# Down projection of a feed-forward: which loads wait behind a split of weights, and the order of the final product

## The chip, the core and the metric

The kernel runs on one core of a Trainium2 chip. The metric is device time in microseconds (us), from the start of the program to its end. Lower is better. The core has TensorE (PE, matrix products), VectorE (DVE), ScalarE (ACT), GpSimd (POOL) and SyncE (SP), each with its own instruction queue that runs in order, and 16 DMA engines that all loads share.

## The reference, cut to what matters

Two layers, each of them a feed-forward, a mixer and a second feed-forward, each followed by a residual and a layer norm, on 512 tokens of width 1024 in float32. A feed-forward is a SwiGLU of width 2816:

```python
def swiglu_ffn(x, w_gu, w_down):
    a, u = jnp.split(x @ w_gu, 2, axis=-1)
    return (jax.nn.silu(a) * u) @ w_down

for l in range(DEPTH):
    x = layer_norm(ALPHA*x + 0.5*swiglu_ffn(x, ffn1_w_gu[l], ffn1_w_down[l]), ln1_g[l], ln1_b[l])
    x = layer_norm(ALPHA*x + hybrid_mixer(x, w_in[l], w_out[l], ...), ln2_g[l], ln2_b[l])
    x = layer_norm(ALPHA*x + 0.5*swiglu_ffn(x, ffn2_w_gu[l], ffn2_w_down[l]), ln3_g[l], ln3_b[l])
```

So there are four feed-forwards, each with a product by `w_down` (2816x1024) at its end: the down projection. The last of them writes the output.

## The kernel before, in words

**Precision.** Every float32 operand is split in a high part (a cast on ACT, L165) and a low part (a subtract on DVE, L166), and every product is three matmuls (`mm3`: high x high on L174, high x low on L175, low x high on L176). The tile names tell what is split: `uh`/`ul` are the two parts of a unit of weights (128x1024), `xh`/`xl` the two parts of an operand from the tokens' side.

**Down projection.** Of the 22 chunks of 128 features in `hT`, 20 go through seven products of blocks instead of eight (a Strassen scheme over two halves of the features, two halves of the tokens and two halves of the 1024 output columns). In the code's names they run in the order p2, p1, p5, p6, p3, p7, p4. Each product has five groups, `seventh` computes one group, and a group is 12 matmuls of 512 columns (two PSUM banks, two chunks of features, three matmuls). The last two chunks, the tail (`down`, `tail(t)`), are ordinary products with their own raw weights. `tail(t)` also calls `norm(t)` for token tile t (0 to 3). In program order: p2, p1, p5, p6, p3, p7, then `tail(0)` and `tail(1)`, then p4 (banks of token tiles 2 and 3), then `tail(2)` and `tail(3)`.

**Weights' side of the seven products.** `R` tiles hold blocks of `w_down`, loaded by SP (L363). The products need sums of blocks, and these sums are made by DMA: after a group of p1, p5, p6 or p3 has been split, POOL issues a load that adds another block onto the same piece of `R` (L374, `accum_op=add`, 512 KB each, 20 in each down projection). The groups of p5 use what p1's groups added, those of p6 what p5's added, those of p4 what p6's added, and those of p7 what p3's added. `R[0,...]` serves p1, p5, p6 and p4; `R[1,...]` serves p3 and p7. p2 uses plain raw tiles (L386).

**Order of loads.** `Weights` holds the items (units of weights) of the whole program in order. `pump` emits splits up to `LOOK` (6) items ahead of the consumer, with 6 unit buffers, so a unit's split waits until the unit six places earlier has been used up by PE. There are two raw tiles; after each item `pump` looks through all later items for the next raw tile to load until two are held. `load_ln` loads gain and shift of the norm (two loads of 512 KB into 128 partitions). SP issues all plain loads in program order. The dependencies between instructions are turned into semaphore waits by the framework.

Of the kernel before, what the change touches and what calls it, by code (L numbers as in the profile page):

```python
# [7 lines left out]
F32 = mybir.dt.float32  # L8
# [10 lines left out]
P = 128  # L19
# [10 lines left out]
GROUPS = 5  # L30
# [2 lines left out]
PAIRS = [(m, min(4, HALF - m)) for m in range(0, HALF, 4)]  # L33
SEVEN = (2, 3, 4, 5, 6, 7, 8, 9, 10)
UBUFS = 6
LOOK = 6
DELAY = (5, 4, 9, 9)
STEPS = ((4, 2, 2), (3, 2, 3), (3, 3, 2), (3, 2, 2))

QA, KA, VA, QR, KR, VR, GR = 0, 512, 640, 768, 1280, 1792, 2304  # L40

NOSYNC = mybir.DependencyInfo(mybir.DependencyClass.NoSync, mybir.DependencyReason.DATA)


class Weights:
# [9 lines left out]
    def pump(self, most=None):  # L55
        while self.emitted < len(self.items) and self.emitted < self.taken + LOOK:
            if most is not None and self.emitted >= most:
                return
            raw, load, pool, cut = self.items[self.emitted]
            if pool is None and self.out >= UBUFS:  # L60
                return
            if raw is not None:
                self.load(raw, load)
            if pool is None:
                self.out += 1
                hi, lo = self.T.units()
            else:
                hi, lo = pool()
            self.ready.append(cut(self.raws.get(raw), hi, lo))
            self.emitted += 1  # L70
            held = sum(self.last[r] >= self.emitted for r in self.raws)
            for r2, l2, _, _ in self.items[self.emitted :]:
                if held == 2:
                    break
                if r2 is not None and r2 not in self.raws:
                    self.load(r2, l2)
                    held += 1
# [20 lines left out]
class Trunk:  # L98
    def __init__(self, tc, ctx):
        self.tc, self.nc = tc, tc.nc  # L100
        self.n = 0
        self.now = 0
        self.pin = True
        self.tasks = []
        self.later = []
        self.halves = 2
        nc = self.nc
        self.base = ctx.enter_context(tc.tile_pool(name="base", bufs=1))
        self.rawp = ctx.enter_context(tc.tile_pool(name="rawp", bufs=2))
        self.unit = ctx.enter_context(tc.tile_pool(name="unit", bufs=UBUFS))  # L110
        self.small = ctx.enter_context(tc.tile_pool(name="small", bufs=3))
        self.psum = ctx.enter_context(tc.tile_pool(name="psum", bufs=8, space=PSUM))
        self.ident = self.base.tile([P, P], F32, name="ident")
        make_identity(nc, self.ident)
        self.mhalf = self.base.tile([P, 8], F32, name="mhalf")
        nc.vector.memset(self.mhalf, -0.5)
        self.xh = self.base.tile([P, KC, SEQ], F32R, name="xh")
        self.xl = self.base.tile([P, KC, SEQ], F32R, name="xl")
        self.Y = self.base.tile([P, NT, D], F32, name="Y")
# [43 lines left out]

    def split(self, hi, lo, src):
        a = self.nc.scalar.copy(hi, src)  # L165
        b = self.nc.vector.tensor_sub(lo, src, hi.bitcast(F32))  # L166
        if self.pin:
            self.tc.keep_in_program_order(a)
            self.tc.keep_in_program_order(b)

    def mm3(self, out, a, b, start, stop, **kw):
        (ah, al), (bh, bl) = a, b
# [11 lines left out]
    def cols_item(self, w, c0, key):  # L184

        def load():
            v = self.raw().rearrange("p (k c) -> p k c", k=KC)
            src = w[:, c0 : c0 + 256].rearrange("(k p) c -> p k c", p=P)
            if self.later is not None:
                self.later.append(lambda: self.nc.sync.dma_start(v[:, :, P:], src[:, :, P:]))  # L190
                for k0 in range(0, KC, KC // (1 if self.later[1:] else 2)):
                    k1 = k0 + KC // (1 if self.later[1:] else 2)
                    self.nc.sync.dma_start(v[:, k0:k1, :P], src[:, k0:k1, :P])
            else:
                self.nc.sync.dma_start(v, src)
            return v

        def cut(c):
            def go(v, hi, lo):
                hv, lv = (t.rearrange("p (k c) -> p k c", k=KC) for t in (hi, lo))  # L200
                src, h = v[:, :, c * P : (c + 1) * P], KC // 2
                if self.halves:
                    self.halves -= 1
                    self.split(hv[:, :h], lv[:, :h], src[:, :h])
                    self.rest = lambda: self.split(hv[:, h:], lv[:, h:], src[:, h:])
                    if not self.halves:
                        self.rest()
                else:
                    self.split(hv, lv, src)
                return hv, lv  # L210
            return go

        return [(key, load, None, cut(c)) for c in range(2)]
# [50 lines left out]
    def rows_item(self, w, r0, key, pools, heads=False):  # L264

        def load():
            v = self.raw().rearrange("p (c n) -> p c n", c=2)
            if heads:
                for kv in range(2):
                    q0 = kv * 256 + r0 // 2  # L270
                    self.nc.sync.dma_start(v[kv * HD : (kv + 1) * HD],
                                           w[q0 : q0 + P, :].rearrange("(c p) n -> p c n", p=HD))
            else:
                self.nc.sync.dma_start(v, w[r0 : r0 + 256, :].rearrange("(c p) n -> p c n", p=P))
            return v

        def cut(c):
            def go(v, hi, lo):
                self.split(hi, lo, v[:, c, :])
                return hi, lo  # L280
            return go

        return [(key, load, pools[c], cut(c)) for c in range(2)]
# [63 lines left out]
    def down_items(self, w, key, tail):  # L347
# [4 lines left out]
        R = {}  # L352
# [5 lines left out]
        def begin(i, m, place, go):  # L358
            def f(*args):
                k0, n = PAIRS[m]  # L360
                pool, tag = place()
                R[i, m] = pool.tile([P, n, 512], F32, tag=tag, name=self.nm("R"), bufs=2)
                self.nc.sync.dma_start(R[i, m], rows(i, i, k0, n))  # L363
                return go(*args)
            return f

        def cut(t, g, *more):
            def go(v, hi, lo):
                hv, lv = (t_.rearrange("p (k c) -> p k c", k=2) for t_ in (hi, lo))
                src = R[t, g // 2][:, g % 2 * 2 : g % 2 * 2 + 2, :]  # L370
                self.split(hv, lv, src)
                for i, j in more:
                    self.tc.keep_in_program_order(
                        self.nc.gpsimd.dma_start(src, rows(i, j, g * 2, 2), accum_op=ALU.add))  # L374
                return hv, lv
            return go
# [94 lines left out]
    def load_ln(self, pool, g, b, tag="ln", bufs=None):  # L471
        kw = {} if bufs is None else {"bufs": bufs}
        gb = pool.tile([P, 2, D], F32, tag=tag, name=self.nm("ln"), **kw)
        self.nc.sync.dma_start(gb[:, 0, :], g.partition_broadcast(P))
        self.nc.sync.dma_start(gb[:, 1, :], b.partition_broadcast(P))
        return gb[:, 0, :], gb[:, 1, :]

    def norm(self, t, halves, gb, out=None, delay=4, scale=(ALPHA, ALPHA)):
# [29 lines left out]
    def ffn(self, g_, b, out=None):  # L508
        nc, tc, W = self.nc, self.tc, self.W
        with ExitStack() as ctx:  # L510
# [147 lines left out]
            pool = self.fpool = ctx.enter_context(tc.tile_pool(name=self.nm("ffnd"), bufs=1))  # L658
            acc = [[self.ps() for _ in range(2)] for _ in range(NT)]

            gb = self.load_ln(pool, g_, b)
            calls = [0]

            def part(m, i, j):
# [5 lines left out]
            def operand(src):  # L670


                calls[0] += 1
                k, h = ((4, 0), (0, 0), (0, 1), (4, 1))[calls[0] % 4 if calls[0] < 20 else 2]
                f = src.shape[1]
                hh, hl = (v[:, k : k + f, h * 256 : (h + 1) * 256] for v in (self.xh, self.xl))
                self.split(hh, hl, src)
                return [(hh[:, q : q + 2], hl[:, q : q + 2]) for q in range(0, f, 2)]
# [35 lines left out]
                for m in ms:  # L714
                    yield from operand(part(m, 1, 1))

            def seventh(banks, u, h, new):

                for i, b_ in enumerate(banks):
                    ts = slice(i * P, (i + 1) * P)  # L720
                    for f in range(2):
                        self.mm3(b_, (h[0][:, f, ts], h[1][:, f, ts]), (u[0][:, f, :], u[1][:, f, :]),
                                 new and f == 0, False, skip_group_check=True)
                self.step()

# [30 lines left out]
            for n, (banks, new, more) in enumerate((  # L756
# [3 lines left out]
                if n == 6:  # L760
                    last = [take() for _ in range(TAIL)]
                    self.pend = []
                    for t in range(2):
                        tail(t)
                for g in range(GROUPS):
                    u, h = take()
                    seventh(banks, u, h, new and g == 0)
                    if more and g == GROUPS - 1:
                        into(banks, *more)
                    W.done(2 if n == 0 and g == 1 else 1)  # L770
            for t in range(2, NT):
                tail(t)


    def big(self, shape, dt=F32):
# [385 lines left out]
```

## Time and profile before

| | us |
|---|---|
| median of three runs | 1786.18 |
| lowest and highest of the three | 1784.37, 1790.02 |
| the profiled execution, its own time | 1784.17 |
| its span, first to last instruction | 1782.4 |
| TensorE busy | 1758.7 |
| VectorE busy | 1414.1 |
| ScalarE busy | 926.9 |

The profile tells when each instruction ran, what ended its wait, and what DMA moved; 1.8 us of the profiled execution lie outside its span. A matmul's shown duration overlaps that of the next, so the pace of TensorE is read from the distance of starts. The granted clock says which of its two levels TensorE ran at: 1.00 is 2.4 GHz.

### The profile page before, as it was taken

What the parts mean: (1) busy time and instruction counts of PE and PEld (TensorE: products, weight loads), DVE (VectorE), ACT (ScalarE), POOL (GpSimd) and SP (SyncE); (2) the same over time, 40 slices, a digit from 0 to 9 for tenths busy, and PEclk for the clock granted to TensorE, in tenths of its full rate; (3) what the DMA queues carried; (4) which work ended last, traced back from release to release, by engine and by line L of the source; (5) the groups of instructions that cost most, each with busy time, mean ns of one, the idle gap of its engine ahead of it and who ended that gap; (6) DMA issues with size and microseconds to landing.
All of it is one profiled execution on the core that took longest, in us unless ns stands there. A gap on an engine that the chain in (4) does not pass through costs nothing.

```text
span 1782.4 us, 29182 instructions
## 1 busy us (share of the span) xinstructions
PE 1758.7 (99%) x11930; PEld 1603.4 (90%) x11930; DVE 1414.1 (79%) x1975; ACT 926.9 (52%) x1456; POOL 181.8 (10%) x152
## 2 busy tenths in 40 slices
PE   9999999999999999999999999999999999999997
PEld 9999987897789999997899999789877899999886
DVE  7888878956757888887988888888567587888886
ACT  5455546478712455555435556454696234555561
POOL 0000023111111000013100000221111110000131
PEclk9999999999999999999999999999999999999999
DMA  6334399222222243279322334972233122334891
GB/s 189 95 104 134 120 248 188 90 84 88 76 74 71 85 129 95 96 246 227 83 84 97 104 95 154 255 146 90 84 95 95 48 95 95 96 101 137 233 180 47
DMA packets 163765, 216.34 MB, mean 121 GB/s; under 512 B 5168, under 2 KB 116528, under 8 KB 163632
## 3 DMA queue, kind: packets, MB, share of 16 engines
q1 hardware_dynamic: 141872, 172.55, 30.2%
q0 software_dynamic: 21760, 41.95, 12.9%
q8 instruction: 93, 1.52, 0.4%
q14 instruction: 40, 0.33, 0.1%
HBM read 212.38 MB, written 2.10 MB: 120 GB/s over the span
## 4 chain that ended last, share of the span: by engine, by line
PE 79%; issue 10%; DMA 4%; DVE 3%; POOL 2%; ACT 1%; POOLq 0%; SPq 0%; DVEq 0%; ACTq 0%
PE ps L176 25%; PE ps L174 25%; PE ps L175 25%; DMA R<-in_ffn_w_down_dram 2%; POOL R L374 1%; DVE ul L166 1%; PE ps L461 1%; DMA raw<-in_ffn_w_gu_dram 1%; POOL sw L932 1%; PE ps L1040 1%; ACT uh L165 1%; PE ps L988 0%; PE ps L1002 0%; PE ps L1036 0%; DVE hT L596 0%
## 5 line engine op out<-in xcount | busy, mean ns | idle before, releaser
L174 PE MATMUL ps<-xh,uh 128*128 128x256 f32 (+1 forms) x1616 | 482.2, 298 | 0.0
L176 PE MATMUL ps<-xh,ul 128*128 128x256 f32 (+1 forms) x1616 | 479.4, 297 | 0.8 <-DVE ul L166 0.7
L175 PE MATMUL ps<-xl,uh 128*128 128x256 f32 (+1 forms) x1616 | 478.5, 296 | 0.2 <-DVE xl L166 0.2
L165 ACT CAST uh<-raw 128x1024 fp32r<-128x1024 f32 (+1 forms) x274 | 237.6, 886 | 229.0 <-PE ps L175 134.4
L174 PE MATMUL ps<-Th,uh 128*128 128x256 f32 x1152 | 319.1, 277 | 0.0
L175 PE MATMUL ps<-Tl,uh 128*128 128x256 f32 x1152 | 318.7, 277 | 0.0
L176 PE MATMUL ps<-Th,ul 128*128 128x256 f32 x1152 | 318.3, 276 | 0.0
L176 PEld LDWEIGHTS ps<-xh,ul 128*128 128x128 f32 x1616 | 307.9, 191 | 9.9 <-DVE ul L166 1.4
L174 PEld LDWEIGHTS ps<-xh,uh 128*128 128x128 f32 x1616 | 307.9, 191 | 9.8 <-issue 1.6
L175 PEld LDWEIGHTS ps<-xl,uh 128*128 128x128 f32 x1616 | 308.0, 191 | 7.9 <-DVE xl L166 0.4
L166 DVE TENSOR_TENSOR ul<-raw,uh 128x1024 fp32r<-128x1024 f32 (+1 forms) x274 | 273.5, 1012 | 42.0 <-ACT uh L165 41.2
L176 PE MATMUL ps<-uh,xl 128*128 128x512 f32 x720 | 283.2, 393 | 9.3 <-DVE xl L166 9.3
L174 PE MATMUL ps<-uh,xh 128*128 128x512 f32 x720 | 285.4, 396 | 0.5 <-ACT xh L165 0.5
L175 PE MATMUL ps<-ul,xh 128*128 128x512 f32 x720 | 282.0, 392 | 0.0
L165 ACT CAST uh<-S 128x1024 fp32r<-128x1024 f32 x144 | 151.1, 1050 | 149.0 <-PE ps L175 145.1
L166 DVE TENSOR_TENSOR ul<-S,uh 128x1024 fp32r<-128x1024 f32 x144 | 175.9, 1222 | 59.7 <-ACT uh L165 59.1
L175 PEld LDWEIGHTS ps<-Tl,uh 128*128 128x128 f32 x1152 | 216.7, 188 | 0.0
L174 PEld LDWEIGHTS ps<-Th,uh 128*128 128x128 f32 x1152 | 216.7, 188 | 0.0
L176 PEld LDWEIGHTS ps<-Th,ul 128*128 128x128 f32 x1152 | 216.3, 188 | 0.0
L374 POOL DMA_DIRECT2D R<-in_ffn_w_down_dram x80 | 97.1, 1217 | 1046.1 <-DVE ul L166 719.6
L165 ACT CAST uh<-R 128x1024 fp32r<-128x1024 f32 x120 | 124.4, 1047 | 125.0 <-DMA R<-in_ffn_w_down_dram 92.9
L166 DVE TENSOR_TENSOR ul<-R,uh 128x1024 fp32r<-128x1024 f32 x120 | 144.7, 1220 | 54.6 <-ACT uh L165 54.4
(143 smaller groups left out, 2372.7 us busy)
## 6 DMA issues: line engine op xcount, KB each, us to landing
raw<-in_ffn_w_gu_dram SPq DMA_DIRECT2D x86, 1024.0 KB, 5.6
R<-in_ffn_w_down_dram POOLq DMA_DIRECT2D x80, 512.0 KB, 8.4
raw<-in_w_in_dram SPq DMA_DIRECT2D x18, 1024.0 KB, 5.3
R<-in_ffn_w_down_dram SPq DMA_DIRECT2D x16, 1024.0 KB, 11.2
raw<-in_ffn_w_down_dram SPq DMA_DIRECT2D x12, 1024.0 KB, 5.4
R<-in_ffn_w_down_dram SPq DMA_DIRECT2D x8, 512.0 KB, 10.5
raw<-in_w_in_dram SPq DMA_DIRECT2D x8, 512.0 KB, 7.9
raw<-in_w_out_dram SPq DMA_DIRECT2D x8, 512.0 KB, 6.1
```

Source lines behind the costliest of these rows:

```text
L165: a = self.nc.scalar.copy(hi, src)
L166: b = self.nc.vector.tensor_sub(lo, src, hi.bitcast(F32))
L174: keep(mm(out, ah, bh, start=start, stop=False, **kw))
L175: keep(mm(out, ah, bl, start=False, stop=False, **kw))
L176: keep(mm(out, al, bh, start=False, stop=stop, **kw))
L374: self.nc.gpsimd.dma_start(src, rows(i, j, g * 2, 2), accum_op=ALU.add))
L461: nc.tensor.transpose(b[:, c * P : (c + 1) * P], src[:, c * P : (c + 1) * P], self.ident)
L932: nc.gpsimd.tensor_mul(sw[:, :n], sw[:, :n], S)
L1040: ins = nc.tensor.matmul(ob[:, o0 : o0 + HD], ST[h][:, n, :], vr[:, n, p * P + h * HD : p * P + (h + 1) * HD], start=n == 0, stop=n == 0 o ...
```

## The change

Loads through `fetch` get a wait on the subtract of a weight split, where `self.pace` is set. `self.pace` is set by the split of the last group of p1, p5, p6 and p4 and by every group of p3 and p7, and it is cleared when a unit of a column item (gate/up weights, or the mixer's first weights) is emitted. Four kinds of loads go through `fetch`: column items, row items (the tail's raw weights), the `R` tiles, and the norm's gain and shift. The look-ahead for raw tiles is cut to the next eight items, and `load_ln` moves from ahead of the seven products to the place ahead of p3. In the final feed-forward, p4 is taken as five units at once, and its five groups run for token tile 2, then `tail(2)`, then for token tile 3, then `tail(3)`; one operand buffer index of that feed-forward changes so that the last operand doesn't wait for the operand two places before it.

```diff
+AHEAD = 8
-            for r2, l2, _, _ in self.items[self.emitted :]:
+            for r2, l2, _, _ in self.items[self.emitted : self.emitted + AHEAD]:
...
     def split(self, hi, lo, src):
         a = self.nc.scalar.copy(hi, src)
-        b = self.nc.vector.tensor_sub(lo, src, hi.bitcast(F32))
+        b = self.low = self.nc.vector.tensor_sub(lo, src, hi.bitcast(F32))
...
+    def fetch(self, dst, src):
+
+        ins = self.nc.sync.dma_start(dst, src)
+        if self.pace is not None:
+            self.tc.add_manual_dep(ins.ins, self.pace.ins.name, SYNC, reason="the queues are for the sums first")
...
-                self.nc.sync.dma_start(v, src)
+                self.fetch(v, src)
...
             def go(v, hi, lo):
+                self.pace = None
...
-                self.nc.sync.dma_start(v, w[r0 : r0 + 256, :].rearrange("(c p) n -> p c n", p=P))
+                self.fetch(v, w[r0 : r0 + 256, :].rearrange("(c p) n -> p c n", p=P))
...
-                self.nc.sync.dma_start(R[i, m], rows(i, i, k0, n))
+                self.fetch(R[i, m], rows(i, i, k0, n))
...
                 self.split(hv, lv, src)
+                if t or g == GROUPS - 1:
+                    self.pace = self.low
...
-        self.nc.sync.dma_start(gb[:, 0, :], g.partition_broadcast(P))
-        self.nc.sync.dma_start(gb[:, 1, :], b.partition_broadcast(P))
+        self.fetch(gb[:, 0, :], g.partition_broadcast(P))
+        self.fetch(gb[:, 1, :], b.partition_broadcast(P))
...
-            gb = self.load_ln(pool, g_, b)
             calls = [0]
...
-                k, h = ((4, 0), (0, 0), (0, 1), (4, 1))[calls[0] % 4 if calls[0] < 20 else 2]
+                k, h = ((4, 0), (0, 0), (0, 1), (4, 1))[calls[0] % 4 if out is not None or calls[0] < 20 else 2]
...
-            def seventh(banks, u, h, new):
+            def seventh(banks, u, h, new, groups=(0, 1)):
 
-                for i, b_ in enumerate(banks):
+                for i in groups:
...
                     for t in range(2):
                         tail(t)
+                    if out is not None:
+                        continue
+                if n == 4:
+                    gb = self.load_ln(pool, g_, b)
...
+            us = [take() for _ in range(GROUPS)] if out is not None else []
             for t in range(2, NT):
+                for u, h in us:
+                    seventh(low, u, h, False, (t - 2,))
                 tail(t)
+            W.done(len(us))
```

SP's queue at the first down projection, before the change; `raw` with `in_ffn_w_down` and 2x1024 is the tail's weights, 8x256 of `in_w_in` the mixer's first weights, `R` with 2x512 first the last piece of `R[0]` and then the three pieces of `R[1]`:

```order
L386 DMA raw_2673<-in_ffn_w_down_dram 128x2x512
L274 DMA raw_2739<-in_ffn_w_down_dram 128x2x1024
L195 DMA raw_2772<-in_w_in_dram 128x8x256
L474 DMA ln_2789<-in_ln_g_dram 128x1024
L475 DMA ln_2789<-in_ln_b_dram 128x1024
L363 DMA R_2828<-in_ffn_w_down_dram 128x2x512
L363 DMA R_2890<-in_ffn_w_down_dram 128x2x512
L363 DMA R_2892<-in_ffn_w_down_dram 128x4x512
L363 DMA R_2894<-in_ffn_w_down_dram 128x4x512
```

The same place of SP's queue after the change:

```order
L398 DMA raw_2673<-in_ffn_w_down_dram 128x2x512
L176 DMA R_2821<-in_ffn_w_down_dram 128x2x512
L176 DMA R_2883<-in_ffn_w_down_dram 128x2x512
L176 DMA R_2885<-in_ffn_w_down_dram 128x4x512
L176 DMA R_2887<-in_ffn_w_down_dram 128x4x512
L176 DMA raw_3123<-in_ffn_w_down_dram 128x2x1024
L176 DMA ln_3183<-in_ln_g_dram 128x1024
L176 DMA ln_3183<-in_ln_b_dram 128x1024
L176 DMA raw_3255<-in_w_in_dram 128x8x256
```

The four `R` loads now stand ahead of the tail's, the norm's and the mixer's loads. The last piece of `R[0]` has no added wait; the three of `R[1]` wait for the split of p1's last group, the tail's load for that of p3's third group, the norm's for p7's first, the mixer's for p7's last.

ACT's queue in p7 of the same down projection, before the change; casts from `R` with `2894`, `2892` and `2890` are the weights of p7's five groups, and the casts from the tail's raw weights stand far earlier (in p1 and in p6):

```order
L165 CAST xh<-hT_145 128x4x256
L165 CAST uh_3184<-R_2894 128x1024
L165 CAST uh_3200<-R_2894 128x1024
L165 CAST hr_3312<-hT_145 128x1024
L165 CAST uh_3219<-R_2892 128x1024
```

And after it, with the same five groups named `2887`, `2885` and `2883`:

```order
L168 CAST xh<-hT_145 128x4x256
L168 CAST uh_3179<-R_2887 128x1024
L168 CAST uh_3271<-raw_3123 128x1024
L168 CAST uh_3287<-raw_3123 128x1024
L168 CAST uh_3198<-R_2887 128x1024
```

The two casts of the tail's weights now stand between the first and the second group of p7, so the second group's cast waits in the queue until the tail's load has landed. DVE's subtracts stand in the same order.

DVE's last rows before the change, where `L485` adds a PSUM half to the residual, `L487` takes its statistics, and `L494` and `L497` normalise; `ps_17118` and `ps_17119` are the halves of token tile 2, `ps_17120` and `ps_17121` those of tile 3:

```order
L485 SCALAR_TENSOR_TENSOR Y<-Y,ps_17119 128x512
L487 BN_STATS st_17833<-Y 128x6
L485 SCALAR_TENSOR_TENSOR Y<-Y,ps_17120 128x512
L489 BN_AGGR mv_17838<-st_17833 128x2
L487 BN_STATS st_17861<-Y 128x6
L491 TENSOR_SCALAR ve_17840<-mv_17838 128x1
L494 SCALAR_TENSOR_TENSOR Y<-Y,mv_17838,ln_17122 128x1024
L485 SCALAR_TENSOR_TENSOR Y<-Y,ps_17121 128x512
L497 SCALAR_TENSOR_TENSOR Y<-Y,rs_17842,ln_17122 128x512 x2
L487 BN_STATS st_17861<-Y 128x6
L489 BN_AGGR mv_17866<-st_17861 128x2
```

And after it, with tile 2 in `ps_17116` and `ps_17117` and tile 3 in `ps_17118` and `ps_17119`:

```order
L497 SCALAR_TENSOR_TENSOR Y<-Y,ps_17117 128x512
L499 BN_STATS st_17803<-Y 128x6
L501 BN_AGGR mv_17808<-st_17803 128x2
L503 TENSOR_SCALAR ve_17810<-mv_17808 128x1
L506 SCALAR_TENSOR_TENSOR Y<-Y,mv_17808,ln_17518 128x1024
L509 SCALAR_TENSOR_TENSOR Y<-Y,rs_17812,ln_17518 128x512 x2
L497 SCALAR_TENSOR_TENSOR Y<-Y,ps_17118 128x512
L499 BN_STATS st_17861<-Y 128x6
L497 SCALAR_TENSOR_TENSOR Y<-Y,ps_17119 128x512
L499 BN_STATS st_17861<-Y 128x6
L501 BN_AGGR mv_17866<-st_17861 128x2
```

Tile 2's norm no longer stands between the instructions of tile 3's. On PE, the five groups and the tail of tile 2 (30 and 12 matmuls) now stand whole ahead of the 42 of tile 3.

## Rows read from the trace of the kernel before

**Rows 1.** The page's first line.

```profile
span 1782.4 us, 29182 instructions
```

**Rows 2.** Who waited for whom, TensorE: us in total, times, longest.

```profile
PE ps L176 <- DVE xl L166: 9.3, 4, 3.2
```

**Rows 3.** TensorE in order of time, first down projection: start, shown duration, operation [idle before].

```profile
270.83 0.39 PE L174 MATMUL ps<-uh,xh 128*128 128x512 f32 x1
271.06 0.39 PE L175 MATMUL ps<-ul,xh 128*128 128x512 f32 x1
274.15 0.50 PE L176 MATMUL ps<-uh,xl 128*128 128x512 f32 x1 [2.70 <-DVE xl L166]
...
275.83 0.63 PE L176 MATMUL ps<-uh,xl 128*128 128x512 f32 x1
276.26 0.63 PE L174 MATMUL ps<-uh,xh 128*128 128x512 f32 x1
...
278.82 0.40 PE L174 MATMUL ps<-uh,xh 128*128 128x512 f32 x1
```

**Rows 4.** The same view at the same place of the other three.

```profile
822.32 0.50 PE L176 MATMUL ps<-uh,xl 128*128 128x512 f32 x1 [2.73 <-DVE xl L166]
...
1156.68 0.79 PE L176 MATMUL ps<-uh,xl 128*128 128x512 f32 x1 [3.19 <-DVE xl L166]
...
1163.08 0.40 PE L176 MATMUL ps<-uh,xl 128*128 128x512 f32 x1
...
1703.89 0.50 PE L176 MATMUL ps<-uh,xl 128*128 128x512 f32 x1 [0.68 <-DVE xl L166]
```

**Rows 5.** Windows, TensorE: length, PE busy, granted clock, DMA share, GB/s.

```profile
268.20:282.00 13.80, 11.10 (x42) 0.88 1.13 205
...
1699.95:1713.75 13.80, 13.12 (x58) 1.00 1.12 203
```

**Rows 6.** ACT and DVE in order of time: first, last and again first down projection.

```profile
271.19 1.04 ACT L165 CAST uh<-R 128x1024 fp32r<-128x1024 f32 x1 [1.50 <-DMA R<-in_ffn_w_down_dram]
...
1700.92 1.05 ACT L165 CAST uh<-R 128x1024 fp32r<-128x1024 f32 x1 [1.48 <-DMA R<-in_ffn_w_down_dram]
...
273.41 0.68 DVE L166 TENSOR_TENSOR xl<-s,xh 128x512 fp32r<-128x512 f32 x1
```

**Rows 7.** SP's issues in order of time, first down projection.

```profile
235.28 0.37 SPq L195 DMA_DIRECT2D raw<-in_w_in_dram  x1
235.69 0.57 SPq L474 DMA_DIRECT2D ln<-in_ln_g_dram  x1
...
236.78 0.56 SPq L363 DMA_DIRECT2D R<-in_ffn_w_down_dram  x1
```

**Rows 8.** A window with plain loads alone, all engines.

```profile
235.00:239.00 4.00, 4.00 (x19) 3.31 (x18) 3.97 (x5) 2.45 (x3) 0.00 (x0) 1.00 1.01 378
```

**Rows 9.** DMA issues at 281.0 to 281.6, 281.0, 237.9 and 238.4: KB each, us to landing.

```profile
raw<-in_w_in_dram SPq DMA_DIRECT2D x2, 512.0 KB, 17.3
...
raw<-in_w_in_dram SPq DMA_DIRECT2D x1, 512.0 KB, 13.4
...
R<-in_ffn_w_down_dram SPq DMA_DIRECT2D x1, 1024.0 KB, 19.8
...
R<-in_ffn_w_down_dram SPq DMA_DIRECT2D x1, 1024.0 KB, 27.1
```

**Rows 10.** DVE and ACT in order of time: p3's third group, the mixer's first weights.

```profile
287.77 1.22 DVE L166 TENSOR_TENSOR ul<-R,uh 128x1024 fp32r<-128x1024 f32 x1
...
319.19 1.05 ACT L165 CAST uh<-raw 128x1024 fp32r<-128x1024 f32 x1 [1.67 <-PE ps L176]
```

**Rows 11.** PE's last matmul, and DVE in tile 3's norm.

```profile
1771.41 0.39 PE L176 MATMUL ps<-uh,hr 128*128 128x512 f32 x1
...
1773.06 0.68 DVE L485 SCALAR_TENSOR_TENSOR Y<-Y,ps 128x512 f32<-128x512 f32 x1
1773.66 1.41 DVE L497 SCALAR_TENSOR_TENSOR Y<-Y,rs,ln 128x512 f32<-128x512 f32 x2
1774.98 0.69 DVE L487 BATCH_NORM_STATS2 st<-Y 128x6 f32<-128x512 f32 x1
```

More of the change, by code (lines that the diff above doesn't have):

```diff
@@ L40 @@
 QA, KA, VA, QR, KR, VR, GR = 0, 512, 640, 768, 1280, 1792, 2304
+SYNC = mybir.DependencyInfo(mybir.DependencyClass.Sync, mybir.DependencyReason.DATA)
 NOSYNC = mybir.DependencyInfo(mybir.DependencyClass.NoSync, mybir.DependencyReason.DATA)
@@ L199, in go @@
             def go(v, hi, lo):
+                self.pace = None
                 hv, lv = (t.rearrange("p (k c) -> p k c", k=KC) for t in (hi, lo))
@@ L715, in operands @@
                     yield from operand(part(m, 1, 1))
-            def seventh(banks, u, h, new):
-                for i, b_ in enumerate(banks):
+            def seventh(banks, u, h, new, groups=(0, 1)):
+                for i in groups:
                     ts = slice(i * P, (i + 1) * P)
                     for f in range(2):
-                        self.mm3(b_, (h[0][:, f, ts], h[1][:, f, ts]), (u[0][:, f, :], u[1][:, f, :]),
+                        self.mm3(banks[i], (h[0][:, f, ts], h[1][:, f, ts]), (u[0][:, f, :], u[1][:, f, :]),
                                  new and f == 0, False, skip_group_check=True)
```

## The prediction

> **What bounds the kernel now.** I read the page first. The span is 1782.4 us [rows 1], TensorE is busy in nearly all of it, and the profiled execution took 1784.17. So what a change of loads can give back is only time in which TensorE waits or runs at a lower clock, and the time after its last matmul. The view of waits comes second: TensorE's only waits of weight are four for a low part made by DVE, 9.3 us together, the longest 3.2 [rows 2]. The order of time shows where: one in each down projection, in the last group of p5. In the first, the starts step by 0.23 us (270.83, 271.06), and then the next start is 274.15, so 3.09 - 0.23 = 2.86 us are lost; the row calls 2.70 of it idle, and the 0.16 more is the shown overlap of two matmuls [rows 3]. The other three show 2.73, 3.19 and 0.68 idle [rows 4], that is 2.89, 3.35 and 0.84 by starts.
>
> Two of the waits cost more than themselves. After the first, starts step by 0.43 (275.83 to 276.26) until 278.82, and the window around it has a granted clock of 0.88, where the one around the fourth wait has 1.00 [rows 3, 5]; a step of 0.43 is the lower of the two levels, 1.2 GHz. From 274.15 to 278.82 there are 13 steps, 4.67 us where 13 x 0.227 = 2.95 would do: 1.72 lost. After the third wait the same stretch is 1156.68 to 1163.08 [rows 4], 15 steps, 6.40 - 3.41 = 2.99 lost.
>
> Why TensorE waits: the low part it lacks is DVE's subtract at 273.41, and ahead of that on DVE stands the subtract of p6's second group, whose cast on ACT began at 271.19 when a block sum had landed [rows 6]. So the chain is: block sum lands, ACT casts, DVE subtracts the weights, DVE subtracts the operand, TensorE goes on. The sums are late because the DMA engines are full: their share is 1.12 to 1.13 while only sums move, at about 203 GB/s [rows 5], where plain loads move 378 GB/s [rows 8].
>
> **The change, part by part.** *Loads moved behind.* Ahead of the sums in SP's queue stood the tail's 1 MB, the next stage's 1 MB (235.28), the norm's two loads of 0.5 MB (from 235.69) and only then the four R loads (236.78) [rows 7]. After the change the last piece of R[0] goes first, R[1] waits for p1's last split, and the other three come behind p3 and p7. R[1]'s 2.5 MB still share the engines with the sums; the norm's 1 MB, the next stage's 1 MB and the competition of the first R piece leave the stretch.
>
> What that is worth is priced by the trace itself. The last down projection has no next stage and lacks its load, and there the same cast begins at 1700.92, which is 1703.89 - 1700.92 = 2.97 before the waiting matmul starts; in the first it is 274.15 - 271.19 = 2.96. The chain behind the cast is equal, and the wait is 0.84 instead of 2.86: 1 MB less on the queue is 2.02 us [rows 3, 4, 6]. By that price the norm's 1 MB and half a MB of R are 3.0 us more; by bytes, 1.57 MB at 378 GB/s is 4.2 us [rows 8]. Together with the next stage's load the sum is earlier by 5.0 to 6.2 us in the first three, by 3.0 to 4.2 in the last. Needed are 2.86, 2.89, 3.35 and 0.84. All four waits should be gone, with at least 1.6 us to spare; I take them as gone, and keep as the other bound that only the 2.02 comes. With them goes the lower clock, since in each of the two places the pace fell behind a wait. Sum: 2.86 + 1.72 + 2.89 + 3.35 + 2.99 + 0.84 = 14.65 us.
>
> *What is late next.* Products follow one another at 12 x 0.227 = 2.72 us a group, and p5's last group begins at 270.83 [rows 3], so p2 began at 232.7, and without the wait p7's first two groups begin at 300.8 and 303.5. The tail's load now waits for p3's third subtract. That one needs the unit buffer of p6's second group, free at 232.7 + 17 x 2.72 = 278.9, so it ends between 281.3 (cast 1.05, subtract 1.22) and 284.4 (where it ended before, 287.77 + 1.22, less the 4.58 of the first place) [rows 10]. How long its 1 MB then takes beside the sums no row shows directly. Two 1 MB loads of R beside sums landed 19.8 and 27.1 us after issues 0.5 us apart, so one took about 8; two loads of 0.5 MB with rows of 512 bytes took 13.4 and, from the median of 17.3, about 21 [rows 9]. The tail's rows are 4 KB, R's 2 KB, so I take 8: it lands by 289 to 292, and the casts and subtracts to p7's second group (2 x 1.05 + 1.05 + 1.2) end by 297, 6 us before 303.5. The other end, 21, is a rival below. The mixer's weights wait for p7's last split, which PE lets happen at about 300; its cast began at 319.19 [rows 10], now 314.6, so 14 us hide a load of 1 MB. The norm's loads have longer still. If one of these covers went, its lateness would stand on TensorE in full. The cut look-ahead changes nothing elsewhere, since gate, up and mixer items carry a new raw tile at least every eight items. The extra semaphore waits stand in SP's queue, which only issues loads.
>
> *Final product.* Matmuls are the same in number. Before, tile 3's last half was ready when TensorE ended, 1771.41 + 0.39 = 1771.80, but its addition began at 1773.06 and its statistics at 1774.98, behind three large operations of tile 2's norm [rows 11]. After, tile 2's halves are ready 48 and 42 matmuls before the end (10.9 and 9.5 us), and its norm is over by then. Tile 3's addition can begin at 1771.85, its statistics at 0.73 later, 1772.58, against 1774.98: 2.40 us, and what follows keeps its length. A bound below: if tile 2's norm still overlapped, 0; I take 2.4, since tile 2's norm is four operations of 0.7, two passes of 1.4 or less and small ones, an estimate of 7 us from these rows' lengths, and it has 9.5. p4's units are all split before the tails of tiles 0 and 1 in either order, so taking five at once waits for nothing new.
>
> Sum: 14.65 + 2.40 = 17.05, and 1784.17 - 17.05 = 1767.1 for an execution like the profiled one. The median of the runs shown lies 2.0 above that execution, so the median should come at 1767.1 to 1769.1; I say 1768.
>
> **The rivals.** *Shrunk, not gone.* Only the next stage's share comes (2.02 us), because R[1] now starts later and shares with later sums. Then 0.84, 0.87, 1.33 and 0.84 stay: 3.9 us, 1771 to 1772, and with one fall of the clock (1.7 to 3.0) up to 1776. For it: R[1]'s 2.5 MB are the largest load and stay in the stretch.
>
> *The loads are not what the sums wait for.* The sums are bound by their own pace, and only the end gains: 1784.17 - 2.4 = 1781.8. Against it: the last down projection's shorter wait. Sums without any plain load move at 203 GB/s, 2.6 us for each 0.5 MB, with the engines full [rows 5]. The Trainium skill (DMA: Bandwidth & Descriptors, section "Anatomy of one DMA — SWDGE (gpsimd) path") fits 2.0 us plus bytes at 436 GB/s for a load that GpSimd issues, an estimate of 1.2 us of moving for 0.5 MB; by that rule the engines would have room beside the sums, and moving the loads would give nothing but the end. The trace does not agree with that pace for these adding loads.
>
> *Slower: the tail's load comes too late.* ACT casts the tail's weights between p7's first and second group, so a late load blocks the queue. If its 1 MB takes 21 us as the mixer's did [rows 9], it lands at 302.3 to 305.4, p7's second group is ready 4.35 us later, 306.7 to 309.8, and TensorE waits 3.2 to 6.3 in each down projection, 13 to 25 in all, plus falls of the clock of up to 3.0 each. With 20 and one fall the time is 1767 + 23 = 1790. It decides from 303.5 - 4.35 - 284.4 = 14.8 us for the load. Against it: only the load of 512-byte rows was that slow, R's was not. The Trainium skill (same page, section "Queues, rings and completion order") says that an engine takes turns between queues packet by packet; by that rule longer rows get a larger share beside the sums. The trace agrees: 8 us for a MB in rows of 2 KB, 21 in rows of 512 bytes.
>
> **How the numbers follow.** All four waits gone 0.66, shrunk 0.20, the end alone 0.06, tail late 0.08. The predicted time is the first's, 1768. Its own range is 1764 to 1771, a spread of runs like that before. To leave out no more than 2 in 10 the range takes in the shrunk case: 1764 to 1776. About 0.3% (5 us) is what a measurement can tell from no change. Faster by more than that: the first two, 0.86. Within it: the end alone, and a tail that is barely late, 0.07. Slower: 0.07.
>
> **What would show it.** In the profile after: no wait of TensorE for a low part in p5's last group; no step of 0.43 there; p6's second cast 1.6 us or more earlier against its matmul's place than needed; SP's issues of R ahead of the tail's; the tail's load landing before p7's second group; tile 3's addition within 0.1 us of the last matmul's end, and the span ending some 2.4 us earlier behind it. I am wrong if TensorE shows a new wait in p7 or at the start of the next stage, or if the wait in p5 stays.

## The result, and the profile after

| | before | after |
|---|---|---|
| median of five runs each on one chip | 1784.69 | 1774.31 |
| lowest and highest | 1781.61, 1790.02 | 1772.27, 1776.58 |
| profiled execution, its own time | 1784.17 | 1773.25 |
| its span | 1782.4 | 1771.5 |

The ratio is 0.9939, with a 95% interval from 0.9919 to 0.9960: faster by 0.6%, some 10.4 us, where 17 were forecast.

The view of waits of the kernel after, TensorE (waited for: us in total, times, longest), beside [rows 2]:

```profile
PE ps L473 <- DVE Y L509: 3.2, 3, 1.7
PE ps L185 <- DVE xl L169: 1.6, 1, 1.6
```

Of the four waits in p5 one is left, and a line that was not among the waits before stands at the top: the transposes of the next stage (L473) wait for the last operation of a norm on DVE (L509). In order of time, the wait that is left is in the first down projection, at the place of [rows 3]; no step of 0.43 follows it:

```profile
271.74 0.39 PE L183 MATMUL ps<-uh,xh 128*128 128x512 f32 x1
271.96 0.39 PE L184 MATMUL ps<-ul,xh 128*128 128x512 f32 x1
273.91 0.50 PE L185 MATMUL ps<-uh,xl 128*128 128x512 f32 x1 [1.56 <-DVE xl L169]
```

It costs 273.91 - 271.96 - 0.23 = 1.72 us by starts. The longest of the new waits, behind the second down projection:

```profile
877.86 0.39 PE L185 MATMUL ps<-uh,xl 128*128 128x512 f32 x1
879.91 0.66 PE L473 MATMUL ps<-ident,Y 128*128 128x128 f32 x4 [1.66 <-DVE Y L509]
```

By starts the three new waits cost 0.33 (first), 1.82 (second) and 1.56 (third): 3.7 us that the forecast lacks. The end, PE's last matmul and DVE in tile 3's norm, beside [rows 11]:

```profile
1762.91 0.39 PE L185 MATMUL ps<-uh,hr 128*128 128x512 f32 x1
1763.34 0.69 DVE L497 SCALAR_TENSOR_TENSOR Y<-Y,ps 128x512 f32<-128x512 f32 x1
1764.06 0.69 DVE L499 BATCH_NORM_STATS2 st<-Y 128x6 f32<-128x512 f32 x1
```

The addition begins 0.04 after PE's end (1762.91 + 0.39), and from there to the end of the span it is 1771.5 - 1763.3 = 8.2 us, where it was 1782.4 - 1771.8 = 10.6.

The accounts of the two profiled executions: waits and slow steps of p5 14.65 less 1.72, gained 12.9; the end 2.4; the new waits -3.7; the first 215 us of the program, ahead of the first down projection, -0.9 (the same matmul starts at 215.9 instead of 215.0). The sum is 10.7, and the spans differ by 10.9.

### The profile page after: what moved, and what is told of

Read it like the earlier page. It is cut to its first block, busy times and chain, and to the rows that moved or that the text cites. A ratio compares the mean times of both kernels' runs of the same rounds, so it can differ in the third digit from the quotient of the medians.

```text
span 1771.5 us, 29190 instructions
## 1 busy us (share of the span) xinstructions
PE 1754.4 (99%) x11930; PEld 1600.7 (90%) x11930; DVE 1412.8 (80%) x1975; ACT 925.2 (52%) x1456; POOL 181.8 (10%) x152
## 3 DMA queue, kind: packets, MB, share of 16 engines
q1 hardware_dynamic: 141872, 172.55, 30.4%
## 5 line engine op out<-in xcount | busy, mean ns | idle before, releaser
L185 PE MATMUL ps<-uh,xl 128*128 128x512 f32 x720 | 281.0, 390 | 1.6 <-DVE xl L169 1.6
L169 DVE TENSOR_TENSOR ul<-R,uh 128x1024 fp32r<-128x1024 f32 x120 | 144.5, 1221 | 55.2 <-ACT uh L168 55.2
```

What stands on the lines that cost most here:

```text
L169: b = self.low = self.nc.vector.tensor_sub(lo, src, hi.bitcast(F32))
L185: keep(mm(out, al, bh, start=False, stop=stop, **kw))
```

## The experiments

What all runs turn on is when block sums land. The seventh sum of a down projection is the weights' side of p6's second group, on which [rows 6] hang, and the twentieth ends p7's weights. This table is worked out from the views of DMA issues and of POOL in order of time (start of an adding load plus its time to landing, less the start of the first one of that down projection) and, for the waits, from the distances of TensorE's starts as above; us, for the first to the fourth down projection.

| | 7th sum lands at | TensorE's wait in p5 | 20th sum lands at |
|---|---|---|---|
| before | 32.0 31.9 32.4 29.9 | 2.86 2.89 3.35 0.84 | 69.5 68.3 69.5 64.3 |
| before, second trace | 32.0 31.9 32.5 28.9 | 2.89 2.81 3.46 0 | 69.1 68.4 70.3 63.6 |
| the end alone | 31.7 31.8 31.9 29.0 | 2.59 2.75 2.87 0 | 68.6 68.2 68.9 63.4 |
| no waits | 31.6 32.4 31.7 28.7 | 2.44 3.33 2.62 0 | 68.4 68.9 68.8 63.1 |
| after | 30.8 28.0 29.0 28.9 | 1.72 0 0 0 | 69.3 68.9 68.7 68.3 |
| after, second trace | 30.0 29.6 29.6 29.7 | 0.88 0.59 0.56 0.62 | 70.1 69.7 70.1 69.0 |
| norm's loads late | 29.9 28.8 29.6 29.1 | 0.82 0 0.53 0 | 66.2 67.1 66.3 66.4 |
| norm's loads early | 30.4 29.5 29.0 30.3 | 1.31 0.43 0 1.22 | 66.4 65.6 66.3 66.8 |
| R on the first split | 27.9 28.4 28.5 28.5 | 0 0 0 0 | 66.7 67.4 67.0 67.2 |
| R free, norm's early | 27.6 28.4 28.7 27.9 | 0 0 0 0 | 63.4 65.4 65.1 64.9 |
| R free | 24.6 25.4 25.9 24.5 | 0 0 0 0 | 63.7 64.5 66.9 64.7 |
| R free, norm's late | 24.5 24.5 26.7 24.3 | 0 0 0 0 | 61.8 61.9 63.0 60.7 |

One number holds in all twelve traces: TensorE's wait is the seventh sum's landing less 29.1, within 0.1 us in each of 23 waits, and nothing where that is below zero. So p5 is decided by the seventh sum alone.

What sets the pace of the sums shows in the same views: from the fourth sum on, POOL issues each one 0.26 to 0.32 us after the landing of the sum three places before it, in every down projection of all twelve traces. Three sums are thus under way at a time. From the fourth on none is held up by the split that it also needs, and a delay of an early sum is handed on to all later ones.

**The end alone.** The kernel before, with p4 of the final feed-forward as in the diff and no other edit.

> The kernel before with only the final p4 run token tile by token tile; no load is moved. Theory (the end is a term of its own, 2.40 us, because tile 2's norm no longer stands between tile 3's instructions): the stretch from PE's last matmul to the span's end shrinks from 10.6 to 8.2 us, the four waits of p5 stay at 9.3 us in total, time 2.4 us below the kernel before, ratio 0.9987. Rival (the end came from the loads): stretch 10.6, no change.

Measured: ratio 0.9986 (0.9977 to 0.9996), 1781.15 to 1783.31. From PE's end at 1765.14 to the end of the span at 1773.3 it is 8.2 us. The term of 2.40 holds, and is independent of the loads. The three waits of p5 are 8.2 us by starts; none of them was followed by slow steps in the traced execution, which is the fastest of twelve (1775.13).

**R free.** The one edit to the kernel after:

```diff
-                self.fetch(R[i, m], rows(i, i, k0, n))
+                self.nc.sync.dma_start(R[i, m], rows(i, i, k0, n))
```

> The changed kernel, with the three R[1] loads issued without a wait, right behind R[0]'s last piece. Theory 'idle engines' (while R[1] waits for p1's last split the DMA engines move little, and every later sum is late by that): in the first down projection the 7th sum lands about 28 us after the first sum's issue instead of 30.8, TensorE's wait in p5 (1.7 us) is gone, the 20th sum lands 2 to 3 us earlier (66 to 67 instead of 69) and TensorE's waits for tile 1's norm (3.2 us in all) shrink to under 1; time 3 to 5 us below the changed kernel, 1769 to 1771. Rival 'R's bytes cost the sums the same wherever they stand': the first sums fall back to about 10 us after issue as before the change, the 7th lands at 30 to 31, the wait in p5 stays at 1.7 or more and the time at 1774.

Measured: ratio 0.9910 (0.9897 to 0.9922), 1766.93 us against 1783.31, and the four runs lie within 0.7 us. That is 2 us below the range expected, and the 7th sum of the first down projection lands 3.4 us earlier than expected. No wait is left in p5 and none for tile 1's norm; the 7th sum is 2.6 to 6.2 us earlier than after. Windows around the first sums, first the kernel after, then R free (length, busy time of PE, PEld, DVE, ACT, POOL, then the granted clock, the DMA share and GB/s):

```profile
239.00:240.00 1.00, 1.00 (x6) 0.81 (x5) 1.00 (x2) 0.93 (x1) 0.00 (x0) 1.00 0.00 0
240.00:241.00 1.00, 1.00 (x6) 0.84 (x5) 1.00 (x2) 1.00 (x2) 0.98 (x1) 1.00 0.00 0
241.00:242.00 1.00, 1.00 (x6) 0.84 (x5) 1.00 (x2) 0.28 (x2) 0.37 (x1) 1.00 0.00 0
...
244.00:245.00 1.00, 1.00 (x7) 0.81 (x6) 1.00 (x2) 0.27 (x1) 0.71 (x1) 1.00 1.10 203
```

```profile
239.00:240.00 1.00, 1.00 (x6) 0.82 (x5) 1.00 (x2) 1.00 (x2) 0.43 (x1) 1.00 0.96 346
240.00:241.00 1.00, 1.00 (x6) 0.83 (x5) 1.00 (x2) 0.62 (x1) 0.92 (x1) 1.00 1.04 399
241.00:242.00 1.00, 1.00 (x6) 0.84 (x5) 1.00 (x2) 0.66 (x2) 0.19 (x1) 1.00 1.04 379
```

For three microseconds of the kernel after the DMA engines move nothing: R[1] waits for p1's last split, and the first sum, issued at 240.02, moves its first bytes after 242. With R free they move 346 to 399 GB/s in that time. The bytes that R leaves there are paid later. SP issues R[1] in the kernel after at

```profile
247.12 2.41 SPq L176 DMA_DIRECT2D R<-in_ffn_w_down_dram  x3
```

and from then on the sums go at half to two thirds of their pace: the third to the seventh land at 251.9, 257.3, 262.6, 266.6 and 270.9, some 5.3 and then 4.1 us apart, where sums alone come every 2.53. POOL's issue of the seventh and its time to landing, which takes in the two sums ahead of it, in the kernel after:

```profile
257.54 1.20 POOL L386 DMA_DIRECT2D R<-in_ffn_w_down_dram  x1 [4.16 <-DVE hT L699]
```

```profile
R<-in_ffn_w_down_dram POOLq DMA_DIRECT2D x1, 512.0 KB, 13.3
```

and with R free:

```profile
255.90 1.20 POOL L386 DMA_DIRECT2D R<-in_ffn_w_down_dram  x1 [1.33 <-DVE xl L169]
```

```profile
R<-in_ffn_w_down_dram POOLq DMA_DIRECT2D x1, 512.0 KB, 8.3
```

**The norm's loads late.** In the kernel after, `load_ln` moves from p3 to behind p7:

```diff
                 if n == 6:
+                    gb = self.load_ln(pool, g_, b)
                     last = [take() for _ in range(TAIL)]
...
-                if n == 4:
-                    gb = self.load_ln(pool, g_, b)
```

> The changed kernel, with the norm's two loads moved from p3 to behind p7, after the next stage's loads. Theory 'last sums' (TensorE's new waits for tile 1's norm come from the last sums, which share the engines with the norm's 1 MB; DVE starts its unbroken run of work when the last sum has been split): the 20th sum lands 2 to 3 us earlier (66 to 67 us after the first sum's issue instead of 69), the waits for tile 1's norm go from 3.2 us to under 1, the wait in p5 stays at 1.7; time 1771. Rival 'DVE's own order' (DVE has its full work there whatever the sums do, and TensorE merely comes sooner): the waits stay at 3.2 and the time at 1774. A second way: the norm's loads are late themselves and norm 0 waits for them, then the waits grow above 3.2.

Measured: ratio 0.9926 (0.9914 to 0.9938), 1769.64 us. No wait of more than 0.1 us for tile 1's norm is left behind a down projection, and the 20th sum is 1.8 to 3.1 us earlier. The waits in p5, 0.82 and 0.53, go with the seventh sum as everywhere. So the last sums do set the new waits. How, the second down projection of the kernel after shows: ACT's casts of p7's last two groups, and the DVE rows with a wait ahead of them from there to the transposes:

```profile
849.83 1.05 ACT L168 CAST uh<-R 128x1024 fp32r<-128x1024 f32 x1 [1.51 <-DMA R<-in_ffn_w_down_dram]
854.58 1.05 ACT L168 CAST uh<-R 128x1024 fp32r<-128x1024 f32 x1 [3.70 <-DMA R<-in_ffn_w_down_dram]
```

```profile
855.66 1.23 DVE L169 TENSOR_TENSOR ul<-R,uh 128x1024 fp32r<-128x1024 f32 x1 [3.52 <-ACT uh L168]
...
878.57 1.28 DVE L509 SCALAR_TENSOR_TENSOR Y<-Y,rs,ln 128x1024 f32<-128x1024 f32 x1
```

DVE stands still for 3.52 us until the twentieth sum is there, and works without a gap from 855.66 to 879.85, through p4's subtracts and both norms; TensorE comes for tile 1 at 878.1. That start is 70.0 us after the first sum's issue (785.65). With the norm's loads late it is 68.3 after (784.14),

```profile
852.43 1.23 DVE L169 TENSOR_TENSOR ul<-R,uh 128x1024 fp32r<-128x1024 f32 x1 [0.53 <-ACT uh L168]
```

and with R free the twentieth sum's subtract begins at 65.7 (848.59 after 782.93).

All traces bear this out. Take the twentieth sum's landing and subtract what TensorE lost in p5 of the same down projection (wait and slow steps). Of the 36 down projections with a next stage, seven have a wait of more than 0.1 us for tile 1's norm, and there the result is 67.4 or more; in the other 29 it is 67.1 or less. The wait is the result less 67.1, within 0.1 us in six of the seven (0.6 more in the second down projection of the second trace of the kernel after).

**The norm's loads early.** In the kernel after, `load_ln` goes back to its old place, without a wait.

> The changed kernel, with the norm's two loads back ahead of the seven products, without a wait, ahead of R[0]'s last piece. Theory 'idle engines': they take time that was idle at 240 to 247, so the 7th sum lands no later than 31.3 us after the first sum's issue (30.8 in the changed kernel), the wait in p5 of the first down projection stays under 2.2 us, no other comes back, and the waits for tile 1's norm go as in the run with the late loads; time 1771. Rival 'bytes are bytes': the 7th sum is 2.0 us later, the wait in the first p5 is 3.7, waits of about 1 to 2 us come back in the other three, time 1775 to 1778.

Measured: ratio 0.9928 (0.9915 to 0.9941), 1770.32 us. No wait for tile 1's norm is left, but three in p5. In the first down projection the 7th sum lands no later for the 1 MB (30.4 against 30.8 and, in the second trace of the kernel after, 30.0). In the second and the fourth it lands 1.5 and 1.4 later than in the first trace of the kernel after, but 0.1 earlier and 0.6 later than in the second, so what the 1 MB costs there isn't shown. The time bears out the first theory; that the other p5 stay free of waits doesn't hold.

**No waits.** The kernel after, with the two lines in `fetch` that add the wait taken out; the order, the look-ahead, the norm's place and the end remain.

> The changed kernel without any wait on a split: only the order of the loads, the cut look-ahead, the place of the norm's loads and the final product are left of the change. Theory 'bytes in the stretch' (the waits on the tail's, the norm's and the next stage's loads give the gain; R's wait takes part of it away): all of the kernel before's loads stand in the stretch again, the 7th sum lands 30 to 32 us after the first one's issue, waits of 2 to 3 us come back in p5 of the first three down projections, time 1777 to 1781, below the kernel before by the end's 2.4 us and little more. Rival 'order is enough' (R first in SP's queue, the others behind it): the 7th sum lands by 27, no wait in p5, time 1767 to 1770 as with R free.

Measured: ratio 0.9993 (0.9983 to 1.0003), 1781.26 us. Three waits in p5, 8.4 us by starts, are back, and each is followed by slow steps. Less the end's part nothing is left: the order of the loads is worth nothing by itself. R free, which has waits on the tail's, the norm's and the next stage's loads alone, has 0.9910, so these waits are worth all that the loads give.

**R free, with the norm's loads early or late.** Both edits above, in one kernel.

> The kernel with R[1] free, and the norm's two loads back at their old place ahead of the seven products, without a wait. 1 MB more in the stretch before the 7th sum, 1 MB less beside the last sums. By the price of 2.0 us for 1 MB, or 3.7 if the 7.4 us between the kernel before (32.0) and the one with R free (24.6) all belong to the norm's and the next stage's 2 MB, the 7th sum lands at 26.6 to 28.3; it may land 4.5 us later than 24.6 before TensorE waits, so: no wait in p5, no wait for tile 1's norm, time 1766 to 1768, the same as with R free. Rival (the norm's place is what matters): the wait in the first p5 comes back with 1 to 2 us, time 1769 to 1771.

> R[1] free and the norm's loads behind p7. Theory: with R free no down projection has more than 0.13 us of lost steps on TensorE, so nothing is left for the loads to give; the same time as with R free, 1766 to 1768, although the 20th sum lands 2 us earlier still. Rival (DVE's and ACT's slack matters elsewhere): 1 to 2 us faster.

Measured: ratio 0.9920 (0.9904 to 0.9935), 1767.30 us early, and 0.9914 (0.9899 to 0.9930), 1766.83 us late, beside 0.9910 for R free. All three are one time. Early, 1 MB brings the 7th sum from 24.6 to 27.6, 3.0 us for 1 MB (3.0, 2.8 and 3.4 in the other three), and no wait comes of it. Nothing is left for the loads to give, and the norm's place is worth something only while R waits.

**R on the first split.** The kernel after, with R[1] waiting for p1's first split (`self.first`, kept by `cut`) instead of the last:

```diff
-                self.fetch(R[i, m], rows(i, i, k0, n))
+                self.fetch(R[i, m], rows(i, i, k0, n), self.first if i else None)
```

> The changed kernel, with R[1]'s loads waiting for p1's first split instead of its last, so that SP issues them near 240.1 instead of 247.1 (with no wait it was 235). Theory 'idle engines' (what R's wait costs is the time in which the DMA engines move nothing, and that ends at 242 when the first sum moves): hardly any of it is given back, the 7th sum lands at 28 to 30.5 us after the first sum's issue (29.2 on average in the changed kernel, 25.1 with R free), some wait in p5 stays, time 1772 to 1774. Rival 'every us of delay counts alike' (R's delay is 7 us shorter out of 12): the 7th sum lands at 26.8 on average, no wait in p5, the time 1768 to 1770.

Measured: ratio 0.9921 (0.9907 to 0.9934), 1769.33 us; the changed kernel beside it on the same chip has 0.9946 (0.9932 to 0.9960). The 7th sum lands at 28.3 on average, as the theory of idle engines has it and not the other, but that is under 29.1, so the waits in p5 go all the same in the traced execution, the fastest of the five (1766.95), and the forecast of the time fails: it lies 3 to 5 us too high. The theory was too narrow as well. R's own loads move sooner after their issue than an adding load does, so more comes back than the time to 242:

```profile
240.00:241.00 1.00, 1.00 (x6) 0.81 (x5) 1.00 (x2) 0.31 (x1) 0.26 (x1) 1.00 0.82 299
241.00:242.00 1.00, 1.00 (x6) 0.84 (x5) 1.00 (x2) 1.00 (x2) 0.84 (x1) 1.00 1.02 375
```

**The changed kernel once more.** A second trace, on the same chip.

> The changed kernel once more, for a second trace and for its time on the same chip as the run beside it. Theory (the waits left are set by the sums' landing, which repeats): the 7th sums land at 28 to 31 us and the 20th at 68 to 70, one wait of 1 to 2 us in the first p5, waits for tile 1's norm of 3 to 4 us in all, no steps of 0.43 us behind them; 1774. Rival (they are chance, as the slow steps are): other waits in other places, differing by over 2 us in all.

Measured: 1774.03 us, lowest 1773.71, highest 1779.85, which is the profiled one. The sums land as expected. The waits in p5 are smaller and in all four down projections, as the seventh sum says; those for tile 1's norm are 1.93, 2.43 and 2.30 by starts, more than expected, and slow steps of 0.43 do follow the last two, some 1.6 us each (granted clock 0.66 from 881 to 886 and from 1216 to 1221). So the new waits are no chance, and their size moves by 3 us from one execution to the other.

**The kernel before once more.** A second trace of it.

> The kernel before once more, for a second trace of it. Theory (a wait of about 2.8 us sometimes makes the clock fall and sometimes not, in another place in each execution): the three waits of 2.7 to 3.1 us stand where they stood, the steps of 0.43 us stand behind other waits than in the first trace or behind none, and the span is shorter by what they cost. Rival (the fall belongs to the place): steps of 0.43 again behind the first and the third wait, 4.7 us in all.

Measured: 1782.52 us, span 1780.7. The waits are 2.89, 2.81 and 3.46 by starts; slow steps follow the first and the second, not the third, and cost 3.0 and 1.6. The row behind the first:

```profile
273.86 0.80 PE L176 MATMUL ps<-uh,xl 128*128 128x512 f32 x1 [2.73 <-DVE xl L166]
274.45 0.63 PE L174 MATMUL ps<-uh,xh 128*128 128x512 f32 x1
274.87 0.63 PE L175 MATMUL ps<-ul,xh 128*128 128x512 f32 x1
```

So the fall doesn't belong to a place, though the first place had it again. The wait of the fourth down projection, 0.84 in [rows 4], is not there in this trace, nor with the end alone, nor with no waits: there the seventh sum lands close to 29.1.

## Why the prediction was right, and where it was not

**The bound and the end: right.** TensorE is held by block sums; the loads in their stretch make them late (no waits against the rest), and the end is a term of its own, 2.4 us.

**The earlier sums: mis-sized, and this is the step that failed.** "Together with the next stage's load the sum is earlier by 5.0 to 6.2 us in the first three, by 3.0 to 4.2 in the last." It was 1.2, 3.9, 3.4 and 1.0 (second trace of both: 2.0, 2.3, 2.9 and -0.8), and needed were 2.9, 2.8, 3.3 and 0.8 by the 29.1. For the loads that were moved the size was rather too small: with R free it is 7.4, 6.5, 6.5 and 5.4, and 1 MB cost 2.8 to 3.4 us where the price was 2.02. What the sum lacked is the price of R's own wait. The working says that R[1] waits for p1's last split and that its 2.5 MB "still share the engines with the sums", and counts that as no change; in fact the engines stood idle while R waited, and the same bytes came back beside the third to the seventh sum. It cost 30.8 - 24.6 = 6.2 us in the first down projection, 2.6, 3.1 and 4.4 in the others (5.4, 4.2, 3.7 and 5.2 by the second trace of the kernel after). The rival "shrunk, not gone" names this very mechanism, "because R[1] now starts later and shares with later sums", and its chance of 0.20 was too low. In the first trace it held in the first down projection alone; in the second, in all four.

**The range held, in part by luck.** The case that the forecast was taken from, all four waits gone, has 1768 and 1764 to 1771, and 1774.3 lies outside. The stated range holds it because it takes in the shrunk case, 1771 to 1776. But that case has 3.9 us of waits, all in p5; in the first trace 1.7 were left there, and 3.7 stood for tile 1's norm, which no rival had.

What sharing costs a sum shows in the packets: from 257.3 to 262.6 the queue of POOL moved 352 and that of SP 350. The Trainium skill (DMA: Bandwidth & Descriptors, section "Queues, rings and completion order") says that a DMA engine takes turns between queues packet by packet; by that rule R and the sums, both with rows of 2 KB, move equal bytes, and the trace agrees. At the 378 GB/s of [rows 8] as many bytes as a sum has take a plain load 1.39 us, so a sum beside R is 2.53 + 1.39 = 3.9 us, an estimate from these two rows; the steps of 4.0 and 4.2 bear it out. In the two of 5.4 and 5.3 more than one sum's bytes moved (0.63 and 0.69 MB, where a sum has 0.52), since three are under way.

**What is late next: one cover was missed.** The list of covers has the tail's, the mixer's and the norm's loads. All of them held: the tail's load was issued at 287.64, 3 us behind the latest time taken, and landed at 296.84, 9.2 us, where 8 were taken and 14.8 would have decided; TensorE has no wait in p7, and that rival is out. It doesn't have DVE between p7's last split and the next stage's transposes. That run of work follows the last sum, which came no earlier (69.3, 68.9 and 68.7 against 69.5, 68.3 and 69.5) while TensorE came sooner by what p5 no longer lost; the tail's and the norm's 2 MB now stand beside sums 15 to 20. The text names "a new wait in p7 or at the start of the next stage" only as a sign of being wrong, without a price; it was 3.7 us, and 6.7 in the second trace.

**The slow steps: right in sum, wrong in kind.** 4.71 us were taken as belonging to two waits. Over four executions whose sums land as before (before twice, the end alone, no waits) seven of the twelve waits of 2.4 to 3.5 us were followed by slow steps, at 1.6 to 3.0 us each: 4.7, 4.6, none and 5.1 us an execution. Of the waits in p5 or for tile 1's norm of 0.3 to 1.93 us, 16 in all traces, none was. It is thus a term that changes from one execution to the next, and it goes with the waits: the runs of the kernel before spread over 5.2 us or more on each chip, those of the three kernels with R free over 0.6, 2.1 and 0.8.

**The median.** The sum was a gain of 17.05. R free gains 16.4 against the kernel before on its own chip (1783.31 less 1766.93), so a gain of that size is there without R's wait, though 4.7 of the sum were the slow steps of one execution; the change as made gains 10.4 and, beside the run on the first split, 9.0.

## What to carry to other kernels

A wait that keeps a load out of a busy stretch is worth something only for bytes that can move to a stretch with room; for bytes that are needed inside the busy stretch it turns idle engines into lost time. Before a wait is added, look in windows of a microsecond at what the DMA engines do while it holds. And when a stall of the leading engine goes, follow each of the other engines to its next common point with the leader: work that starts with the same late transfer as before has now less time.

The fastest kernels here are the ones changed with R[1] left without a wait: 0.9910 of the kernel before (0.9897 to 0.9922), and with the norm's loads early or late the same within the intervals, where the change as made has 0.9939 and 0.9946 in its two comparisons.

## What was not expected of the hardware

With engines full, adding loads of 512 KB land 2.53 us apart, 207 GB/s, while plain loads in the same kernel move 378 to 399 GB/s. An adding load issued while the engines are idle moves nothing for 2 us (240.02 to 242) and, with two more issued 2.2 and 3.4 us behind it, lands after 6.0. Beside a plain load with the same rows of 2 KB the adding loads have 130 GB/s and so has the plain load (0.69 and 0.68 MB from 257.3 to 262.6). TensorE's clock fell to the lower level behind nine of fourteen waits of 2.3 to 3.5 us and stayed up behind the others, of the same length at the same place.
